# A 2x2 average pool: every transfer split into even and odd partitions on two DMA queues

## The chip, the cores and the metric

The kernel runs on one core of a Trainium2 chip. The metric is the device time of one execution in microseconds (us), lower is better. The engines that matter are DVE (vector), ACT (scalar), SP (which here only issues transfers) and the 16 DMA engines that move all bytes. SP and ACT each own one queue of transfers; both queues feed the same 16 DMA engines.

## The reference

The input is 32 x 128 x 256 x 256 in float32 (1074 MB), the window and the stride are 2, and the output is 32 x 128 x 128 x 128 (268 MB). Each output is the mean of a 2x2 window:

```python
for i in range(h_out):
    for j in range(w_out):
        window = x[:, :, i*stride:i*stride+kernel_size, j*stride:j*stride+kernel_size].copy()
        output[:, :, i, j] = np.mean(window, axis=(2, 3))
```

## The kernel before

Two input rows (2 KB) make one output row (512 B); call this a unit. There are 4096 units per partition. 32 groups of 127 units are worked off, each as four tiles of 31 or 32 units, and 32 units are left for the tail. There are two input buffers and one result buffer. DVE adds the two rows, then the neighbouring columns; ACT multiplies by 0.25. All loads and the group stores are on SP. A group's store is issued after the first load of the next group.

```python
IN_UNITS = 32
GROUP = 127
    def pool(it, dst, cuts):
        nc.vector.tensor_add(out=it[:, :, 0:w], in0=it[:, :, 0:w], in1=it[:, :, w:])
        a = 0
        for g in cuts:
            d, v = dst[:, a : a + g], it[:, a : a + g]
            nc.vector.tensor_add(out=d, in0=v[:, :, 0:w:2], in1=v[:, :, 1:w:2])
            nc.scalar.mul(out=d, in_=d, mul=0.25)
            a += g
    # ... cut: groups, pieces
        for i, (a, g) in enumerate(pieces):
            t = in_pool.tile([P, IN_UNITS, 2 * w], f32, name="in_tile")      # bufs=2
            nc.sync.dma_start(out=t[:, :g], in_=xt[:, a : a + g])
            if i == 0 and last:
                nc.sync.dma_start(out=last[0], in_=last[1])
            pool(t[:, :g], res[:, base + a : base + a + g], [g] if i < 3 else [g - 8, 8])
        last = (ot, res[:, base : base + GROUP])
    # ... cut: the tail, 32 units in cuts of 16, 8, 8; loads on SP, its three stores on ACT
```

## Time and profile before

| | before |
|---|---|
| time, median | 3115.3 us (3113.6 to 3117.5, 4 runs) |
| profiled span | 3113.1 us |
| bytes moved | 1342.25 MB, 431 GB/s over the span |
| DVE, ACT busy | 54%, 15% |
| SP queue's packets | 99.8% of 16 engines' span |

These are lines of the page of the kernel before: the span, busy time, the busy share of the DMA engines in 40 equal slices (9 is 90% or more), the queues (packets, MB, share of 16 engines' span; q1 is SP's queue, q10 is ACT's), and the chain of waits that ended last.

```profile
span 3113.1 us, 927 instructions
DVE 1681.9 (54%) x294; ACT 467.7 (15%) x164; POOL 0.2 (0%) x4
DMA  9999999999999999999999999999999999999999
...
q1 hardware_dynamic: 23472, 1340.09, 99.8%
q10 hardware_dynamic: 432, 2.10, 0.2%
...
DMA 69%; DVE 26%; ACT 4%; SPq 0%; issue 0%; DVEq 0%
```

Between 25 and 3050 us the DMA engines are idle for 0.5 us in all (16 engines' mean, from the packet records), so the kernel is bound by what they move. The trace also has a record of every packet (one row of one transfer). A 64 KiB packet took 2418 ns in the median, one of 65,024 B 2399, one of 8 KiB 309. All three are about 8.5 ns plus the bytes at 27.2 B/ns. That agrees with the Trainium skill ("DMA: Bandwidth & Descriptors", section "Where 436 GB/s comes from"), which gives 435.2 GB/s for 16 ports: 16 times 27.2. At that rate the bytes alone take 3084 us. The rest of the span, 29 us, is about 11 us of the 8.5 ns per packet, 1.5 us of completion packets (9 ns each, by which a transfer reports its end), 2 us before the first packets (they start at 1.7 to 2.9 us), and about 15 us in packets that took over 15 ns more than this formula. (The parts add to 1 to 2 us too much, because records of one engine overlap by a few ns.) I call the last kind slow packets; their time is always what they took above the formula. A count over the trace shows where they are: 9.1 us in each engine's last row of a store and 4.9 us in the load rows that start within 1.5 us of the store's end, summed over all engines and divided by 16. They sit at the change from a store to the next load.

The end of the program, from the timeline of before (start, duration, engine, line, operation, destination and source, count, and in brackets the idle time before it and what ended it):

```profile
3062.00 1.28 SPq L105 DMA_DIRECT2D in_tile<-in_x_dram  x3
3062.00 3.62 ACT L65 ACTIVATE res<-res 128x4096 f32<-128x4096 f32 x1 [15.74 <-DVE res L64]
3068.10 8.69 DVE L60 TENSOR_TENSOR in_tile<-in_tile 128x8192 f32<-128x8192 f32 x1 [6.13 <-DMA in_tile<-in_x_dram]
...
3080.29 3.71 ACT L65 ACTIVATE res<-res 128x3072 f32<-128x3072 f32 x2 [14.67 <-DVE res L64]
3081.31 4.42 DVE L60 TENSOR_TENSOR in_tile<-in_tile 128x4096 f32<-128x4096 f32 x1
```

The three tail loads are issued at 3062, 18 us before ACT scales the last full tile. DVE starts that last full tile at 3068.10, and the program ends 45.0 us later. I use this start as the mark between steady state and tail.

### The profile page before, as it was taken

Reading aid. Unit: us, or ns where it says so; the run is one execution under the profiler, and the core shown is the slowest. Engines: PE = TensorE matmul, PEld = TensorE weight load, DVE = VectorE, ACT = ScalarE, POOL = GpSimd, SP = SyncE. Lnnn points to the kernel's source line nnn. Section 1 sums busy time; section 2 is a strip of 40 time slices with the busy share of each in tenths; the row PEclk is TensorE's granted clock in tenths of the full one; section 3 lists DMA queues with packets and bytes.
Section 4 is the critical chain, followed back from the end, with each engine's and each line's share of the span. In section 5 each row is a group of like instructions: output and inputs, shape, how many; then the busy total and the mean of one; then the engine's idle time right before and its main releaser. Section 6 shows DMA issues by size and latency. Waiting matters only on the chain.

```text
span 3113.1 us, 927 instructions
## 1 busy us (share of the span) xinstructions
DVE 1681.9 (54%) x294; ACT 467.7 (15%) x164; POOL 0.2 (0%) x4
## 2 busy tenths in 40 slices
DVE  5556555565555565555655556555565555655556
ACT  1111111111111111111111111111111111111111
POOL 0000000000000000000000000000000000000000
DMA  9999999999999999999999999999999999999999
GB/s 428 427 438 429 439 430 430 427 440 427 433 436 429 428 437 430 431 427 439 429 428 436 432 429 430 437 429 428 428 427 439 432 427 439 429 437 433 429 427 417
DMA packets 23911, 1342.25 MB, mean 431 GB/s; under 512 B 2656, under 2 KB 2656, under 8 KB 2912
## 3 DMA queue, kind: packets, MB, share of 16 engines
q1 hardware_dynamic: 23472, 1340.09, 99.8%
q10 hardware_dynamic: 432, 2.10, 0.2%
q14 instruction: 7, 0.06, 0.0%
HBM read 1073.74 MB, written 268.44 MB: 431 GB/s over the span
## 4 chain that ended last, share of the span: by engine, by line
DMA 69%; DVE 26%; ACT 4%; SPq 0%; issue 0%; DVEq 0%
DMA in_tile<-in_x_dram 69%; DVE in_tile L60 18%; DVE res L64 8%; ACT res L65 4%; SPq L88 0%; DVE in_tile L64 0%; DVEq L64 0%; ACT in_tile L65 0%; SPq L86 0%
## 5 line engine op out<-in xcount | busy, mean ns | idle before, releaser
L60 DVE TENSOR_TENSOR in_tile<-in_tile 128x8192 f32<-128x8192 f32 (+2 forms) x131 | 1113.0, 8497 | 1402.1 <-DMA in_tile<-in_x_dram 1402.1
L65 ACT ACTIVATE res<-res 128x4096 f32<-128x4096 f32 (+3 forms) x160 | 462.4, 2909 | 2619.6 <-DVE res L64 2619.6
L64 DVE TENSOR_TENSOR res<-in_tile 128x4096 f32<-128x4096 f32 (+3 forms) x160 | 564.4, 3544 | 10.8 <-DVE in_tile L60 0.5
L65 ACT ACTIVATE in_tile<-in_tile 128x1024 f32<-128x1024 f32 (+1 forms) x3 | 4.0, 1341 | 8.0 <-DVE in_tile L64 8.0
L64 DVE TENSOR_TENSOR in_tile<-in_tile 128x1024 f32<-128x1024 f32 (+1 forms) x3 | 4.7, 1581 | 0.1
L65 ACT ACT_TABLE_LOAD x1 | 1.3, 1283 | 0.7 <-PEq L191 0.7
L191 POOL MEMSET const-bfloat16-1.0<- 128x1 bf16 x1 | 0.1, 102 | 0.0
L191 POOL MEMSET const-uint8-127<- 128x1 uint8 x1 | 0.1, 102 | 0.0
L191 POOL MEMSET const-float32-0.0<- 128x1 f32 x1 | 0.1, 99 | 0.2 <-issue 0.2
L191 POOL MEMSET const-float32-1.0<- 128x1 f32 x1 | 0.1, 99 | 0.0
## 6 DMA issues: line engine op xcount, KB each, us to landing
out_dram<-res SPq DMA_DIRECT2D x32, 8128.0 KB, 22.0
in_tile<-in_x_dram SPq DMA_DIRECT2D x32, 7936.0 KB, 24.8
in_tile<-in_x_dram SPq DMA_DIRECT2D x1, 4096.0 KB, 15.8
in_tile<-in_x_dram SPq DMA_DIRECT2D x2, 2048.0 KB, 22.7
in_tile<-in_x_dram SPq DMA_DIRECT2D x96, 41.2
out_dram<-in_tile ACTq DMA_DIRECT2D x1, 1024.0 KB, 19.6
out_dram<-in_tile ACTq DMA_DIRECT2D x2, 512.0 KB, 17.2
```

Source lines behind the costliest of these rows:

```text
L60: nc.vector.tensor_add(out=it[:, :, 0:w], in0=it[:, :, 0:w], in1=it[:, :, w:])
L64: nc.vector.tensor_add(out=d, in0=v[:, :, 0:w:2], in1=v[:, :, 1:w:2])
L65: nc.scalar.mul(out=d, in_=d, mul=0.25)
L191: nc = _bacc.Bacc("TRN2", target_bir_lowering=False, num_devices=1)
```

## The change

Each transfer is issued as two: even partitions on SP, odd partitions on ACT. The intent is that two queues keep the DMA engines fed better than one. A hand-made order makes both queues issue everything in the same sequence. The tail is cut into 16 and 16 units, with one store at its end. In the code cuts, "..." marks lines left out, and some remarks after # are mine.

```diff
+    def move(dst, src):
+        nc.sync.dma_start(out=dst[0::2], in_=src[0::2])
+        nc.scalar.dma_start(out=dst[1::2], in_=src[1::2])
...
+    ctx.enter_context(tc.manual_schedule())
+    def load(j):
+        if j < len(jobs):
+            src, g, _ = jobs[j]
+            tiles[j] = new_in()[:, :g]
+            move(tiles[j], src)
+    load(0)
+    load(1)
+    for j, (_, g, dst) in enumerate(jobs):
+        it = tiles.pop(j)
+        rows(it)
+        if j % 4 < 3:
+            cols(it, dst)
+            load(j + 2)
+            scale(dst)
+        else:
+            for a, b in ((0, g - 8), (g - 8, g)):
+                cols(it[:, a:b], dst[:, a:b])
+                scale(dst[:, a:b])
+            if j + 1 < len(jobs):
+                move(*stores[j // 4])
+                load(j + 2)
...
+    for a, b in cuts:                       # the tail: two cuts of 16 units
+        move(it[:, a:b], xt[:, a:b])
+    move(*stores[-1])
+    for a, b in cuts:
+        rows(it[:, a:b])
+        cols(it[:, a:b], to[:, a:b])
+        scale(to[:, a:b])
+    move(ot, to[:, :rest])
```

More of the change, by code (lines that the diff above doesn't have):

```diff
@@ L57, in _pool_2x2, with new_in, rows, cols @@
     res = out_pool.tile([P, GROUP + FIRST, w_out], f32, name="res")
-    def pool(it, dst, cuts):
-        nc.vector.tensor_add(out=it[:, :, 0:w], in0=it[:, :, 0:w], in1=it[:, :, w:])
-        a = 0
-        for g in cuts:
-            d, v = dst[:, a : a + g], it[:, a : a + g]
-            nc.vector.tensor_add(out=d, in0=v[:, :, 0:w:2], in1=v[:, :, 1:w:2])
-            nc.scalar.mul(out=d, in_=d, mul=0.25)
-            a += g
-    groups, rest = divmod(units, GROUP)
-    if rest == 0:
-        groups, rest = groups - 1, GROUP
-    last = None
+    def new_in():
+        return in_pool.tile([P, IN_UNITS, 2 * w], f32, name="in_tile")
+    def move(dst, src):
+        nc.sync.dma_start(out=dst[0::2], in_=src[0::2])
+        nc.scalar.dma_start(out=dst[1::2], in_=src[1::2])
+    def rows(it):
+        nc.vector.tensor_add(out=it[:, :, 0:w], in0=it[:, :, 0:w], in1=it[:, :, w:])
+    def cols(it, dst):
+        nc.vector.tensor_add(out=dst, in0=it[:, :, 0:w:2], in1=it[:, :, 1:w:2])
+    def scale(dst):
+        nc.scalar.mul(out=dst, in_=dst, mul=0.25)
+    groups, rest = divmod(units - 1, GROUP)
+    rest += 1
+    assert rest <= IN_UNITS, rest
+    jobs, stores = [], []
     for k in range(groups):
@@ L83, in _pool_2x2 @@
             pieces = [(3 * IN_UNITS, FIRST)] + [(a - FIRST, g) for a, g in spans]
-        for i, (a, g) in enumerate(pieces):
-            t = in_pool.tile([P, IN_UNITS, 2 * w], f32, name="in_tile")
-            nc.sync.dma_start(out=t[:, :g], in_=xt[:, a : a + g])
-            if i == 0 and last:
-                nc.sync.dma_start(out=last[0], in_=last[1])
-            pool(t[:, :g], res[:, base + a : base + a + g], [g] if i < 3 else [g - 8, 8])
-        last = (ot, res[:, base : base + GROUP])
@@ L94, in _pool_2x2 @@
-    r0 = groups * GROUP * P
-    while rest:
-        n = min(rest, IN_UNITS)
-        t = in_pool.tile([P, IN_UNITS, 2 * w], f32, name="in_tile")
-        tout = in_pool.tile([P, IN_UNITS, 2 * w], f32, name="in_tile")
-        to = tout[:].rearrange("p g f -> p (g f)").rearrange("p (g f) -> p g f", f=w_out)
-        cuts = [n // 2, n // 4, n - n // 2 - n // 4] if n >= 8 else [n]
-        a, parts = 0, []
-        for g in cuts:
-            xt = xv[r0 : r0 + g * P].rearrange("(p g) f -> p g f", p=P)
-            ot = ov[r0 : r0 + g * P].rearrange("(p g) f -> p g f", p=P)
-            nc.sync.dma_start(out=t[:, a : a + g], in_=xt)
-            parts.append((ot, a, g))
-            a += g
-            r0 += g * P
-        rest -= n
-        if rest == 0:
-            nc.sync.dma_start(out=last[0], in_=last[1])
-        for ot, a, g in parts:
-            pool(t[:, a : a + g], to[:, a : a + g], [g])
-            nc.scalar.dma_start(out=ot, in_=to[:, a : a + g])
+        jobs += [(xt[:, a : a + g], g, res[:, base + a : base + a + g]) for a, g in pieces]
@@ new lines, in _pool_2x2 @@
+        stores.append((ot, res[:, base : base + GROUP]))
+    ctx.enter_context(tc.manual_schedule())
+    tiles = {}
+    def load(j):
[19 more added lines that the diff above has]
+                load(j + 2)
@@ new lines, in _pool_2x2 @@
+    r0 = groups * GROUP * P
+    xt = xv[r0 : r0 + rest * P].rearrange("(p g) f -> p g f", p=P)
+    ot = ov[r0 : r0 + rest * P].rearrange("(p g) f -> p g f", p=P)
+    it, tout = new_in(), new_in()
+    to = tout[:].rearrange("p g f -> p (g f)").rearrange("p (g f) -> p g f", f=w_out)
+    half = rest - rest // 2
+    cuts = [(0, half), (half, rest)] if rest > 1 else [(0, rest)]
+    for a, b in cuts:
[5 more added lines that the diff above has]
+        scale(to[:, a:b])
```

## The prediction

> **What bounds the kernel.** The 16 DMA engines. The page's slices show them at 90% or more throughout, and the queue table gives the SP queue's packets 99.8% of 16 engines' span. DVE is busy 54%, ACT 15%. The chain of waits is 69% DMA. Packet durations recorded in the trace are 2418 ns for 64 KiB (median), 2399 for 65,024 B, 309 for 8 KiB: about 8.5 ns plus bytes at 27.2 B/ns. The Trainium skill ("DMA: Bandwidth & Descriptors", "Where 436 GB/s comes from") states 435.2 GB/s for 16 ports, and the trace agrees: 1342.25 MB at that rate are an estimated 3084 us of the 3113 us span. The remaining 29 us are about 12 us of fixed cost per packet, and about 15 us (store packets 9, load packets 6) in slow packets that sit at each group's change from the store to the next load; the others run at full rate. No queueing gap is left to fill.
>
> **What the change moves.** Each 128-row transfer becomes two of 64 rows, even on SP, odd on ACT. The packets (rows) keep size and number, so bytes over engines is unchanged. The same page ("Issuing engines are not separate DMA queues") says that transfers of both queues run on the same 16 engines. The before trace shows this in its tail: there ACT-queue stores of 8 KiB rows alternate with SP-queue packets of 65,024 B, each keeping its own 309 or 2399 ns. Two queues share an engine's time, they do not add to it. Even and odd rows each spread over all partitions, so I expect no engine or port to be overloaded. Added: about 165 more transfers with 16 completion packets of 9 ns each, 1.5 us over 16 engines. DMA issues on ACT (about 0.35 us each) fit in its 85% idle time. The one gain possible in the steady state: with a second queue an engine may have other work during the store-to-load change, so part of the 15 us may go (my guess 0 to 10, 4 in the middle). A group period should stay near the 96.0 us read from the timeline.
>
> **The tail loses.** ACT now issues in program order: the odd halves of the last loads stand behind the scalings of the last full tile. Before, all last loads were issued at 3062 and DMA ran on from 3067.5. Now only the even half (4.2 MB, 9.7 us) is there, ending about 3077; ACT reaches its issue at 3082 to 3084, and data starts some 2.3 us later (as at the kernel's start: issue at 0.7, first packet at 3.0). That idles the engines 7 to 9 us. Then the odd loads share the engines with SP's even store; the second half arrives about 3104, then 4.4+2.3+1.9 us of compute and one last 2.1 MB store (4.8 us), not hidden any more. Estimated tail: +8 to +10 us. All of it is on the critical path.
>
> **Sum.** 3116.3 - 4 + 1.5 + 7 (shaded, issue order may be kinder) = about 3120 us. Range 3100 to 3131. Faster by over 2%: 0.02; within 2%: 0.95; slower by over 2%: 0.03.
>
> **What would show it.** Right: 64 KiB packets still near 2418 ns; each queue near 50% of the engines; group period 95.7 to 96.1; a DMA dip between 3077 and 3086. The step on the change-over is right if the excess of the slow packets falls below 15 us.
>
> **What would make it wrong.** Row-to-engine assignment of a 64-row strided transfer that makes engines collide on a port (packets well above 2418 ns: much slower). The two queues drifting apart, so that tiles complete late and the 6 us slack of DVE per tile vanishes. Or two queues hiding the per-packet fixed cost as well: then 3095 to 3100.

The passage cut from it gave a delay from a transfer's issue to its first packet that the trace doesn't show: at the kernel's start the issue is at 0.73 us and the engines' first packets start at 1.7 to 2.9 us.

## The result, and the profile after

| | before | after |
|---|---|---|
| time, median | 3115.3 us | 3135.7 us (3134.8 to 3136.5, 4 runs) |
| ratio, 95% interval | | 1.0065 (1.0048 to 1.0082) |
| profiled span | 3113.1 us | 3132.9 us |
| last full tile starts | 3068.1 | 3077.1 |
| from there to the end | 45.0 | 55.9 |

The change made the kernel about 20 us slower, within 2% but outside the range I gave.

The same lines of the page of the changed kernel:

```profile
span 3132.9 us, 1398 instructions
DVE 1681.7 (54%) x292; ACT 467.5 (15%) x163; POOL 0.2 (0%) x4
DMA  9999999999999999999999999999999999999998
...
q10 hardware_dynamic: 13040, 671.10, 50.0%
q1 hardware_dynamic: 13040, 671.10, 49.7%
...
DMA 69%; DVE 26%; ACT 4%; ACTq 1%; issue 0%; DVEq 0%
```

The queues share the engines half and half. The rate did not rise, and the last slice now falls under 90%. DVE and ACT do the same work as before.

The 19.8 us of span split cleanly at the mark: 9.0 us were lost before it and 10.9 after it.

**The tail.** These are lines of the changed kernel's timeline; the first is from SP's own, where the two tail loads of SP stand alone.

```profile
3070.91 1.11 SPq L65 DMA_DIRECT2D in_tile<-in_x_dram  x2
```

```profile
3077.09 8.69 DVE L69 TENSOR_TENSOR in_tile<-in_tile 128x8192 f32<-128x8192 f32 x1 [6.21 <-DMA in_tile<-in_x_dram]
3085.89 4.49 DVE L72 TENSOR_TENSOR res<-in_tile 128x3072 f32<-128x3072 f32 x2
3089.28 2.76 ACT L75 ACTIVATE res<-res 128x3072 f32<-128x3072 f32 x1 [14.75 <-DVE res L72]
3090.47 1.13 ACTq L66 DMA_DIRECT2D in_tile<-in_x_dram  x2
...
3114.37 2.29 DVE L72 TENSOR_TENSOR in_tile<-in_tile 128x2048 f32<-128x2048 f32 x1 [7.89 <-DMA in_tile<-in_x_dram]
...
3125.30 0.54 ACTq L66 DMA_DIRECT2D out_dram<-in_tile  x1
```

SP issues its halves of the tail loads at 3070.91, ACT only at 3090.47, because in its program they stand behind the scalings of the last full tile, and those wait for DVE. The windows view shows what the DMA engines did meanwhile (columns: stretch, length, busy time of DVE, ACT and POOL with counts, TensorE clock, DMA share, GB/s). A packet counts in the stretch in which it starts, so a share can pass 1. First two stretches of before, in which the same work is done, then two of after:

```profile
3077.00:3085.00 8.00, 8.00 (x3) 3.71 (x2) 0.00 (x0) 1.00 1.00 426
3085.00:3093.00 8.00, 7.93 (x5) 2.97 (x2) 0.00 (x0) 1.00 1.07 460
```

```profile
3077.00:3088.00 11.00, 10.81 (x2) 0.00 (x0) 0.00 (x0) 1.00 0.77 334
3088.00:3093.00 5.00, 2.38 (x2) 3.71 (x2) 0.00 (x0) 1.00 0.37 105
```

The engines ran at 77% and then 37%. Idle time of the 16 engines in the tail, up to the last data packet, is 10.0 us against 1.0 us before, by the packet records: 6.2 us until ACT's loads come, and 3.4 us before the last store, whose rows are computed late.

**The steady state.** From the second group's first add to the 32nd's, a group takes 96.67 us in the mean against 96.39 before (30 intervals: 99.54 to 2999.55, and 99.02 to 2990.82). That is 8.2 us over the run:

```profile
99.02 8.43 DVE L60 TENSOR_TENSOR in_tile<-in_tile 128x7936 f32<-128x7936 f32 x1 [5.53 <-DMA in_tile<-in_x_dram]
2990.82 8.43 DVE L60 TENSOR_TENSOR in_tile<-in_tile 128x7936 f32<-128x7936 f32 x1 [5.46 <-DMA in_tile<-in_x_dram]
```

```profile
99.54 8.43 DVE L69 TENSOR_TENSOR in_tile<-in_tile 128x7936 f32<-128x7936 f32 x1 [5.52 <-DMA in_tile<-in_x_dram]
2999.55 8.42 DVE L69 TENSOR_TENSOR in_tile<-in_tile 128x7936 f32<-128x7936 f32 x1 [5.47 <-DMA in_tile<-in_x_dram]
```

A 64 KiB packet still takes 2418 ns in the median. The loss is in slow packets, 22.2 us against 15.2, and in twice as many completion packets, 2.8 us against 1.5. Of the slow packets, 13.6 us (before 9.1) are last store rows and 6.1 us (before 4.9) load rows next to them.

The records do not name the engine, but chained end to start they give an engine's sequence (where several records fit within some 50 ns, one of them is taken). This is one chain around a store's end in each kernel (us from the span's start; S is SP's queue, A is ACT's; o a store row, l a load row, * a completion; a number is the duration in ns where it is over 40 ns above the formula):

```
before  109.8So 112.2So 114.6So2733 117.3S* 117.3Sl 119.8Sl 122.2Sl
after   108.0So 110.4Ao 112.9So 115.3Ao3431 118.7S* 118.7A* 118.7Sl 121.1Al 123.6Sl
```

The two queues take turns row by row, so an engine still moves store rows and then load rows, as before; which rows of a tile it carries, the records do not show. They keep in step: in the changed kernel SP's half of each of the first 127 tiles ends 2.3 to 2.4 us, one row, before ACT's. The last store row of every engine is therefore ACT's. It is slow in both chains, and slower after.

### The profile page after: what moved, and what is told of

Its sections match the earlier page's. It is cut to its first block, busy times and chain, and to the rows that moved or that the text cites. A ratio compares the mean times of both kernels' runs of the same rounds, so it can differ in the third digit from the quotient of the medians.

```text
span 3132.9 us, 1398 instructions
## 1 busy us (share of the span) xinstructions
DVE 1681.7 (54%) x292; ACT 467.5 (15%) x163; POOL 0.2 (0%) x4
## 4 chain that ended last, share of the span: by engine, by line
DMA 69%; DVE 26%; ACT 4%; ACTq 1%; issue 0%; DVEq 0%
DMA in_tile<-in_x_dram 69%; DVE in_tile L69 18%; DVE res L72 8%; ACT res L75 4%; ACTq L66 1%; DVE in_tile L72 0%; ACT in_tile L75 0%; DVEq L72 0%; DVEq L69 0%
## 6 DMA issues: line engine op xcount, KB each, us to landing
in_tile<-in_x_dram SPq DMA_DIRECT2D x2, 2048.0 KB, 12.9
```

## The experiments

My theory after the result: the tail loss is ACT's late issue, and the steady-state loss comes from the second queue. Rivals for the latter: twice the number of transfers, or the new order.

Slow packets below are those between 25 and 3050 us of the span that took over 15 ns more than 8.5 ns plus bytes at 27.2 B/ns, as a sum divided by 16. They come from one profiled run each, and single runs of one kernel differ by 3 us or more, so the medians decide and the counts explain.

| kernel | median us | ratio to before (95%) | last full tile starts | slow packets us | completion packets us |
|---|---|---|---|---|---|
| before | | | 3068.1 | 15.2 | 1.5 |
| e3: whole, one queue, new order | 3115.2 | 0.9996 (0.9983-1.0008) | 3068.5 | 15.1 | 1.4 |
| e1: split, one queue | 3115.4 | 0.9997 (0.9985-1.0010) | 3072.2 | 17.5 | 2.9 |
| e2: split, two queues, tail repaired | 3124.4 | 1.0022 (1.0008-1.0035) | 3078.7 | 23.0 | 2.8 |
| e5: only stores split | 3119.7 | 1.0006 (0.9993-1.0019) | 3074.6 | 19.9 | 1.7 |
| changed kernel | 3135.7 | 1.0065 (1.0048-1.0082) | 3077.1 | 22.2 | 2.8 |

The kernel before ran at a median of 3117.7 to 3117.9 in the rounds of e1 to e10, a little above its first four runs.

### e1: both halves on one queue

```diff
         nc.sync.dma_start(out=dst[0::2], in_=src[0::2])
-        nc.scalar.dma_start(out=dst[1::2], in_=src[1::2])
+        nc.sync.dma_start(out=dst[1::2], in_=src[1::2])
```

> The changed kernel with both halves of every transfer on the SP queue: as many transfers and completion packets, one queue. Theory Q (the second queue makes the store-to-load changes dearer): about 3117 us, the last full tile's first add starts near 3069 us (before 3068.1, changed 3077.1), slow store packets of 65,024 B cost about 9 us over 16 engines as before. Theory N (twice the transfers of half the rows cost it, whatever the queue): last full tile near 3077 us, total near 3125, slow store packets about 14 us as in the changed kernel. Both: the tail after that start is about 45 us as before, since SP never waits for the scaling before it issues the last loads.

3115.4 us. Twice the transfers of half the rows cost nothing that the runs resolve, so the medians decide for theory Q. The trace alone would not: its mark lies between the two forecasts, and its slow store rows took 12.9 us, nearer to theory N's 14 than to theory Q's 9. The profiled run was the slowest of the five (3118.2), which may explain it in part.

### e2: the tail loads issued in time

```diff
             tiles[j] = new_in()[:, :g]
             move(tiles[j], src)
+        elif j == len(jobs):                # from the second last tile, before its scaling
+            tiles[j] = new_in()
+            for a, b in cuts:
+                move(tiles[j][:, a:b], xt[:, a:b])
 ...
-    for a, b in cuts:
-        move(it[:, a:b], xt[:, a:b])
     move(*stores[-1])
+    it = tiles.pop(len(jobs))
```

> The changed kernel, only the last loads issued (on both queues) before the scalings of the last two full tiles. Theory T (the tail loss is ACT's late issue): time from the last full tile's first add to the end falls from 55.8 to 45-46 us, idle of the DMA engines there from 10 to about 1 us, total about 3125 us. Rival (sharing of the engines and the one uncovered last store cost it): stays at 52-56 us, total 3131 to 3136. The last full tile still starts near 3077.

3124.4 us, 11.3 below the changed kernel. Lines of its timeline, then of its windows view:

```profile
3072.49 1.11 SPq L65 DMA_DIRECT2D in_tile<-in_x_dram  x2
3072.49 1.38 ACTq L66 DMA_DIRECT2D in_tile<-in_x_dram  x2
...
3078.67 8.69 DVE L69 TENSOR_TENSOR in_tile<-in_tile 128x8192 f32<-128x8192 f32 x1 [6.21 <-DMA in_tile<-in_x_dram]
```

```profile
3077.00:3088.00 11.00, 9.22 (x2) 0.54 (x1) 0.00 (x0) 1.00 1.00 429
3088.00:3093.00 5.00, 5.00 (x3) 2.14 (x1) 0.00 (x0) 1.00 0.97 419
```

Both queues issue at 3072.49, the DMA engines stay full, and from the mark to the end it takes 3123.0 - 3078.7 = 44.3 us, as before. The tail loss was the late issue on ACT; nothing of it is left over. The uncovered last store, still there in e2, costs nothing visible.

### e3: whole transfers on one queue, in the new order

```diff
-        nc.sync.dma_start(out=dst[0::2], in_=src[0::2])
-        nc.scalar.dma_start(out=dst[1::2], in_=src[1::2])
+        nc.sync.dma_start(out=dst, in_=src)
```

> The changed kernel with whole 128-row transfers on SP: only its hand-made order and its other cuts of the tail are left. If order and cuts are harmless (my theory): 3114 to 3117 us, last full tile near 3068, slow packets 15 to 16 us in all. Rival (the manual order costs the 9 us of the steady state): about 3124 us, last full tile near 3077.

3115.2 us, and the last full tile starts at 3068.47. The new order and the new cuts of the tail are free. With e1 this leaves the second queue: all five runs of e2 (3122.7 to 3124.8) lie above all runs of e1 and e3 (3114.5 to 3118.2), and the medians differ by 9 us. The records of e3 and e2 account for it: 7.9 us more slow packets and 1.4 us more completion packets, 9.3 of the 9.6 us between the profiled spans. That ACT issues late in the loop too is not the cause: between 25 and 3050 us the engines are idle for 2.1 us in e2 and 0.7 in e3. Against the kernel before in the same rounds, the medians put e2 6.7 us higher.

### e4: stores whole on SP, loads on both queues

```diff
-                move(*stores[j // 4])       # on top of e2
+                nc.sync.dma_start(out=stores[j // 4][0], in_=stores[j // 4][1])
```

> As e2 (tail repaired), but the 31 group stores inside the loop go whole on SP; loads stay split over both queues. Theory S (two rings that end a store on each engine make the change-over dearer): last full tile near 3069-3071, total about 3117-3119, slow store packets near 9 us. Rival L (split loads alone do it): as e2, near 3077 and 3125. Rival D (loads on ACT's ring overtake the store on SP's ring, so reads and writes mix for a whole store): slower than e2, many more slow packets, DVE waiting longer for the tile after a store.

3373.1 us, ratio 1.0822 (1.0807 to 1.0837): rival D. Lines of its timeline around the first group's store:

```profile
96.75 0.35 SPq L128 DMA_DIRECT2D out_dram<-res  x1
...
149.59 8.69 DVE L69 TENSOR_TENSOR in_tile<-in_tile 128x8192 f32<-128x8192 f32 x1 [37.20 <-DMA in_tile<-in_x_dram]
158.38 4.43 DVE L72 TENSOR_TENSOR res<-in_tile 128x4096 f32<-128x4096 f32 x1
162.72 8.69 DVE L69 TENSOR_TENSOR in_tile<-in_tile 128x8192 f32<-128x8192 f32 x1
162.83 0.50 ACTq L66 DMA_DIRECT2D in_tile<-in_x_dram  x1
```

```profile
140.93 8.69 DVE L69 TENSOR_TENSOR in_tile<-in_tile 128x8192 f32<-128x8192 f32 x1 [28.63 <-DMA in_tile<-in_x_dram]
```

The second fence is the same tile in the changed kernel. In e4 ACT's queue has no store in it, so its odd rows of two tiles take turns with SP's eight store rows per engine, while the even rows of the first tile wait behind them. DVE then waits 37.2 us, finds two tiles ready at once (the add at 162.72 shows no wait), and frees a buffer late. The DMA engines stand idle about 212 us before the last full tile, by the packet records; with 61 us of slow packets (24 in e2) that makes up the loss. So stores on one queue must not hold up half of a tile while the other queue runs ahead. That every transfer must be split does not follow, as e5 shows.

### e5: only the stores split

```diff
-            move(tiles[j], src)             # on top of e2
+            nc.sync.dma_start(out=tiles[j], in_=src)
```

> As e2 (tail repaired) but the 127 loads in the loop go whole on SP; only the stores are split, even rows on SP, odd rows on ACT. Rings stay in step at the start of a store, but the loads behind the store go on one ring only. Theory S (a store that ends on two rings is what costs): near e2, 3123 to 3125 us, slow store packets about 15 us. Theory L (it is the loads behind it that come over two rings): near e1 and e3, 3115 to 3118 us. Either way no tile waits for a whole store as in e4.

3119.7 us lies between e3 and e2, and so do its slow packets. Its interval overlaps those of both, so neither theory S nor theory L is shown. It looks as if each side gave about half, but that is not shown. It does show that loads on one queue and stores on both do no harm like that of e4.

### e6 and e7: twice as many changes from store to load

```diff
+        c = 63 if base == 0 else 32
+        halves.append((1, (ot[:, :c], res[:, base : base + c])))
-        stores.append((ot, res[:, base : base + GROUP]))
+        stores.append((ot[:, c:], res[:, base + c : base + GROUP]))
 ...
             scale(dst)
+            if j % 4 == halves[j // 4][0]:
+                move(*halves[j // 4][1])
```

e6 is e3 with this edit, e7 is e2 with it.

> e3 (whole transfers on SP) with each group's store cut in two, sent after the second and after the fourth tile: 64 changes from store to load in place of 32. Theory: each change costs a fixed time, about 15.4 us / 32 = 0.48 us of slow packets and idle on one queue, so +15 us, +2.2 for 4096 more packets at 8.5 ns and +0.3 for completions: about 3133 us, slow packets and idle about 31 us. Rival (the slow packets belong to the bytes stored, not to the changes): +2.5 us only, 3118.

> e2 (all transfers split over two queues, tail repaired) with the same cut stores as e6. If the second queue's cost sits at the changes, its distance to the one-queue twin doubles: e2 is 9 us above e3, so this is about 18 us above e6, near 3150. Rival (the second queue costs the same everywhere, per packet or per transfer): distance stays about 9 us, near 3142 if e6 is at 3133.

e6 took 3117.2 us (3114.1 to 3128.8), ratio 1.0005 (0.9991 to 1.0018). e7 took 3128.6 us (3122.4 to 3134.7), ratio 1.0039 (1.0027 to 1.0051). My theory of a fixed cost per change fell: 15 us were due in e6, and no loss is resolved. Its rival's 3118, which counts only the additional packets, fits. The slow packets sum to 13.6 us in e6 and 24.3 in e7, about as in e3 and e2, although there are twice as many changes. They also moved: in e6 and e7 the slow ones are the last load rows before some of the stores, and no store row is slow (0.0 and 0.1 us). The distance between two queues and one is 11 us here, against 9; it did not double. The runs of e6 and e7 scatter widely and overlap, so this distance is known to about 6 us only (my estimate from their spread). The edit also puts half of each store between other loads, so it changes more than the number of changes.

### e8: contiguous halves on the two queues

```diff
-        nc.sync.dma_start(out=dst[0::2], in_=src[0::2])       # on top of e2
-        nc.scalar.dma_start(out=dst[1::2], in_=src[1::2])
+        nc.sync.dma_start(out=dst[0:64], in_=src[0:64])
+        nc.scalar.dma_start(out=dst[64:128], in_=src[64:128])
```

> e2 with rows 0 to 63 on SP and 64 to 127 on ACT in place of even and odd rows. If the even/odd split keeps each row on the engine that it has in a whole transfer and that is why it costs nearly nothing, contiguous halves spread otherwise and engines meet on the same part of the on-chip memory: 64 KiB packets well above 2418 ns, over 3200 us. Rival (any split over 16 engines is as good): as e2, 3123 to 3125, packets 2418 ns.

The four runs took 4766 to 5043 us. They are unsteady; even the fastest is 53% above the median of before in its rounds. A stretch of its windows view:

```profile
1000.00:1500.00 500.00, 166.73 (x29) 46.97 (x16) 0.00 (x0) 1.00 0.99 261
```

The engines are busy 99% of the time and move 261 GB/s: the packets take longer. In the whole run a 64 KiB packet takes 3909 ns in the mean (median 3808), against 2426 before. So the even and odd choice of the change is not cosmetic: it leaves the packet time alone, while halves do not. That rows of a contiguous half meet on the same part of the on-chip memory is my reading; no run here tests it against, say, a cause on the DRAM side. The Trainium skill ("DMA: Bandwidth & Descriptors", section "The descriptor swizzle") says that in a 128-row transfer each engine serves its own port, but that section gives no assignment for 64 rows, and the records do not show which engine carried which row.

### e9 and e10: no stores in the loop

```diff
-                move(*stores[j // 4])
```

e9 is e3 with this edit, e10 is e2 with it. Their outputs are wrong, which doesn't matter for the times.

> e3 (whole transfers on SP) without the 31 group stores inside the loop: most of the output is not written, a wrong result on purpose. 257.8 MB less: at 27.2 B/ns and 8.5 ns per packet about 595 us less, and the 15 us of slow packets at the changes gone: about 2505 us. It serves as the one-queue twin of e10.

> e2 (all transfers split over two queues, tail repaired) without the same 31 stores, wrong on purpose. If the second queue costs only where a store ends and loads follow, this is e9 plus about 1 us of completion packets: a distance of 0 to 3 us. Rival (two queues slow the loads themselves, or drift apart in them): the distance of e2 to e3 shrinks only with the time, to about 7 us.

e9 took 2510.2 us (2510.0 to 2510.5) and e10 2511.5 us (2511.3 to 2512.0). From the pages of e9 and e10, in this order:

```profile
span 2508.5 us, 854 instructions
...
q1 hardware_dynamic: 19008, 1084.17, 100.0%
```

```profile
span 2509.5 us, 1243 instructions
...
q1 hardware_dynamic: 10560, 542.09, 50.0%
q10 hardware_dynamic: 10560, 542.09, 49.9%
```

The distance is 1.3 us, and the completion packets alone are 1.2 us more (2.4 against 1.2). Slow packets fall to 1.9 and 2.5 us. So for loads alone two queues cost no more than these packets. The cost of the second queue in the steady state needs the stores. In the traces of the changed kernel and of e2 the slow packets sit at the change from store to load. A fixed cost per change is not supported, though: in e7 the distance did not double. The spread of the runs almost vanishes too.

## Why the prediction was wrong

- **What bounds the kernel: right.** But for the changed kernel's tail, the DMA engines are busy throughout in both kernels, and two queues add no rate. A 64 KiB packet stays at 2418 ns, and each queue has half of the engines. The Trainium skill ("DMA: Bandwidth & Descriptors", section "Issuing engines are not separate DMA queues") says so, and the traces agree.
- **The tail: right in mechanism, a little low in size.** I worked out 8 to 10 us and put 7 into the sum, for the chance of a kinder order. Measured: 10.9 us from the mark to the end, and 11.3 us when e2 takes it away. Most of the error here was the shading.
- **The step that failed: "The one gain possible in the steady state: with a second queue an engine may have other work during the store-to-load change, so part of the 15 us may go".** I put it at -4 us. It has the opposite sign: slow packets rose from 15.2 to 22.2 us. At the change the other queue's row is taken in turn, as the chain shows, but the rows there got slower. e1 and e3 show that neither the number of transfers nor the order does it, and e9 with e10 that it needs stores.
- **Completion packets, +1.5 us: right.** The records show +1.4 (e1, which has them too, is not resolvably slower in its runs).
- **The sum.** For the steady state I predicted -4 + 1.5 = -2.5 us, measured were +9.0; for the tail +7, measured +10.9. The misses add to 15.4 us; from 3120 to 3135.7 it is 15.7. That they agree so well is in part luck: the sum started from 3116.3, not 3115.3, and gives 3120.8 before rounding, and spans differ a little from times.
- **The group period.** I took 96.0 us from one group; the mean of before is 96.4, so my band of 95.7 to 96.1 could not have tested anything.
- **Drift of the queues**, which I feared, did not occur: SP's and ACT's halves end one row apart in all of the first 127 tiles. Slow packets do make the tile after a store late (relative to the group's start 2.9 us later than before after the first store, 1.0 us in the mean), but DVE still waits about 4 us or more before every such tile, so the delay is covered.

What stays open is why a second queue makes the packets at a change slower, and why cutting the stores moves the slow ones from the store's last rows to the loads before. No experiment settles the mechanism inside the memory or the engines. None of the kernels with a right result is clearly faster than the kernel before; e1, e3, e5 and e6 tie with it.

## What to carry to other kernels

When packet records show each DMA engine working back to back, as here, look for bytes or for pauses before you try a second queue; here it had nothing to fill. An engine that both computes and issues transfers issues them in program order, so place early every load that must not wait for its arithmetic, above all in the tail. If transfers must be split over two queues, see that neither queue can run ahead with half of a tile, and test the partition pattern: even and odd rows cost 0.2 to 0.3% here with the tail repaired, halves over 50%, splitting loads but not stores 8%, and splitting stores but not loads nothing that was resolved.

## What the Trainium skill lacked or had wrong

- "DMA: Bandwidth & Descriptors", "Rules for kernel authors", says of two transfers to disjoint partition halves not to bother, since they serialize. It gives no size and does not tell even and odd rows from contiguous halves. Here contiguous halves on two queues took 4766 to 5043 us against 3118, and even and odd rows 3124 (e8, e2). This is a point on that row of the page, not on the whole skill.
- The same page, "Queues, rings and completion order", says that an engine drains a packet of typically 9 to 17 descriptors from one queue before it switches. Here the engines switch after every row of 64 KiB: the queues' halves of a tile end one row, 2.3 to 2.4 us, apart. The records do not show how many descriptors such a row is, so this need not contradict the page.
- No page tells what stores among loads cost beyond their bytes: 15 us of slow packets over 32 groups with one queue and 23 with two, against 2 without stores (e3, e2, e9 and e10).
